# Low parts of every second weight unit by an accumulating DMA, and the C heads' softmax weights turned by VectorE and DRAM

## The chip, the cores and the metric

The kernel runs on one core of a Trainium2 chip. The metric is the device time of one execution in microseconds (us); the time before is 1841.37 us, the median of three runs (1841.23 to 1842.32). The engines are named as in the profile: PE is TensorE (PEld its weight loads), DVE is VectorE, ACT is ScalarE, POOL is GpSimd, SP is SyncE, which issues most DMAs. Each engine works through its own instructions strictly in order.

## The reference

One layer of a hybrid decoder trunk on 512 tokens of 2048 channels, all in float32, cut to what matters:

```python
h = rms_norm(x, norm1_g)
proj = h @ w_in                        # 30 tiles of 128 columns
# A: 8 heads of dilated attention; B: conv module, 512 channels (GLU, causal
#    depthwise conv of 31 taps, LayerNorm, swish); C: 16 query heads over 2 kv heads
out_b = conformer_conv(bu, bg, ...)
cq, ck = rms_norm per head
out_c = band_attention(cq, ck, cv, window 128, sinks)   # p = exp(s - max); o = p @ v / (sum p + sink)
x = x + concat(out_a, out_b, out_c) @ w_out
x = x + (silu(h2 @ w_gate) * (h2 @ w_up)) @ w_down      # h2 = rms_norm(x, norm2_g)
```

## The kernel before, in words

Activations lie transposed: channels on the 128 partitions, the 512 tokens along the free axis. Every large product is made of three products of TensorE in a rounded float32 format (`mm3`): high part of the weights by high part of the activations, high by low, and low by high. So each weight is cut into a high part `wh` and a low part `wl`, and so are the activations (`hh`, `hl` for the normed input, `mh`, `ml` for the mixed rows).

Weights come in *units* of 128 x 1024 (512 KB). Units 0 to 62 are the input projection (0 to 10 the first four column tiles, then two units for each of 26 tiles in the order of `PROJ`), the next 32 the output projection; the gate, up and down products follow. A unit goes through four steps. SyncE loads it into one of seven raw buffers (`pump`, tile `w`). ScalarE casts it to `wh`, and VectorE subtracts, `wl = w - wh` (`split_up_to`, `lows_now`); `wh` and `wl` have three buffers each. TensorE uses it: 8 slices of three matmuls, 24 in all. `next_unit()`, which the use of unit u begins with, asks for the cut of unit u+2 (`SPLIT_AHEAD`). The subtraction is deferred to a place inside the unit (`lows_now` after the fourth slice), and there, too, raw buffers are given back (`release`), one step late, and loads for them issued.

The projections set the clock of everything else: `project(name)` makes one column tile from two units and calls `ticks.tick()` after every second slice, eight ticks in a projection. `Ticks.after(n, fn)` puts a step n ticks ahead, so the order of all engines' instructions is written out by hand in ticks: the attention heads' steps, the convolution's taps on VectorE (`tap`, one multiply-add each, spaced by `TAP_TICKS` ticks for the four channel blocks), the norms. The output projection goes on ticking, and the LayerNorm of the convolution stands at tick `T_LN` = 244. The 26 projections make 208 ticks.

A C head (there are 16, in eight pairs `c0` to `c7`, started six ticks apart) goes through these steps, by the entries of `C_TICKS`: scores on TensorE into two banks of PSUM (`c0s`), masking and row maximum on VectorE (`pack`), exponentials on ScalarE into an SBUF tile `c0e` of 128 queries by 4 blocks of 128 keys (`packed_exps`), the sums (`packed_norm`), four transposes on TensorE into a bank `c0t` (`packed_flip`), the cut into a high part `c0hp` on ScalarE and a low part `c0lp` on VectorE, eight selects on GpSimd that spread both over masked tiles `c0ph`, `c0pl` (`spread_out`), and the weighing with the values on TensorE into `c0o` (`weigh`), then the copies out (`mix_c`).

Attention's V tiles are laid out without TensorE already (`do_v`): VectorE turns 32 x 32 blocks, four DMAs write them to DRAM, one reads them back.

Of the kernel before, what the change touches and what calls it, by code (L numbers as in the profile page):

```python
# [9 lines left out]
F32 = mybir.dt.float32  # L10
# [3 lines left out]
AF = mybir.ActivationFunctionType  # L14
ALU = mybir.AluOpType

P = 128
T = 512
NT = T // P
# [12 lines left out]

OUT_ORDER = (list(range(16)), [n + o for n in range(6) for o in (0, 8)] + [6, 7, 14, 15])

TAP_TICKS = (1.2, 1.3, 1.6, 1.6)
T_LN = 244
T_GLU = 14


SD, KD, VD, EV = 9, 6, 12, 1  # L40


C_TICKS = (1, 6, 2, 2, 2, 3, 5, 1, 4)
A_TICKS = (0, 8, 2, 1, 3, 1, 3, 1, 5)


# [2 lines left out]
ROWS = "c0 c1 c2 c4 c5 c3 c7 c6 a0 a1 b2 b1 b0 b3 a2 a3".split()  # L49

N_SLOTS = 73

RAW_PLAIN = "22b sb 21a 22a 11 sa 12".split()
RAW_BUFS = 8
# [62 lines left out]
def kernel(ctx: ExitStack, tc: tile.TileContext, xT, wi, wo, wgu, wd, cst_in, outT):  # L117
    nc = tc.nc
    cp = ctx.enter_context(tc.tile_pool(name="consts", bufs=1))
    wp = ctx.enter_context(tc.tile_pool(name="weights", bufs=1))  # L120
    sp = ctx.enter_context(tc.tile_pool(name="slots", bufs=N_SLOTS))
    ctx.enter_context(tc.manual_schedule())
# [13 lines left out]
    ticks = Ticks()  # L136

    def slot(name, dt=F32, cols=T):
        return sp.tile([P, cols], dt, name=name, tag="s")

    def bank(name, cols=T, pool="banks"):
        return psum[pool].tile([P, cols], F32, name=name, tag="b")


    units = [wi[0][:, :TH], wi[0][:, TH:T], wi[0][:, T:], wi[1][:, :T], wi[1][:, T:]] + [wi[u] for u in range(2, 2 * N_IN)]
# [14 lines left out]
    def drop(key):  # L160
        for buf in [b for b, k in held.items() if k == key]:
            held.pop(buf)
        return raws.pop(key)
# [42 lines left out]
    for t, (g, r) in enumerate(DOWN):  # L206
# [7 lines left out]
        for k in ("21A", "11A", "21B", "11B", "22A", "22B", "12A", "12B"):  # L214
            c = k[2]
# [17 lines left out]
    at = {"entry": 0, "split": 0, "use": 0}  # L233

    def pump(limit, most=99, eng=nc.sync):
        while at["entry"] < len(entries) and len(raws) < limit and entries[at["entry"]][0] not in held and most:
            most -= 1
            buf, key, parts = entries[at["entry"]]
            size = [part.shape[-1] * (part.shape[1] if len(part.shape) == 3 else 1) for part in parts]
            t, o = take(buf, key, sum(size)), 0  # L240
            for part, n in zip(parts, size):
                to = t[:, o:o + n]
                eng.dma_start(to.rearrange("p (n f) -> p n f", n=part.shape[1]) if len(part.shape) == 3 else to, part)
                o += n
            at["entry"] += 1


    lows, late_lows = [], []
# [8 lines left out]
    def lows_now():  # L257
        if lows and cooling:
            release()
            pump(RAW_EARLY if at["use"] <= 20 else RAW_BUFS)  # L260
        while lows:
            fn, *args = lows.pop(0)
            fn(*args)  # L263
        if late_lows and not cooling:
            pump(RAW_EARLY if at["use"] <= 20 else RAW_BUFS)

    def split_up_to(i):
        while at["split"] <= min(i, len(works) - 1):
            key, last, eng = works[at["split"]]
            of = [b for b, k in held.items() if k == key]  # L270
            t, n = drop(key) if last else raws[key]
            if cooling:
                held.update((b, None) for b in of)
                cool.extend(of)
            u = at["split"]
            hi = wp.tile([P, 1024], F32R, name=f"wh{u}", tag="hi", bufs=SPLIT_BUFS)
            lo = wp.tile([P, 1024], F32R, name=f"wl{u}", tag="lo", bufs=SPLIT_BUFS)
            if eng == "moves":

                near = psum["high"].tile([P, 1024], F32R, name=f"wn{u}", tag="h")  # L280
                src = t[:, :n].rearrange("p (n f c) -> p f n c", n=4, c=P)
                by = lambda x: x[:, :n].rearrange("p (f n c) -> p f n c", n=4, c=P)
                nc.scalar.copy(by(near), src)
                nc.scalar.copy(by(hi), src)
                nc.vector.tensor_sub(by(lo), src, by(near).bitcast(F32))
            elif eng or "high" not in psum:
                eng = eng or nc.vector

                (nc.vector.tensor_copy if u == 0 else nc.scalar.copy)(hi[:, :n], t[:, :n])  # L289
                lows.append((eng.tensor_sub, lo[:, :n], t[:, :n], hi[:, :n].bitcast(F32)))  # L290
                if not late_lows:
                    lows_now()
            else:
                near = psum["high"].tile([P, 1024], F32R, name=f"wn{u}", tag="h")
                nc.scalar.copy(near[:, :n], t[:, :n])
                nc.scalar.copy(hi[:, :n], t[:, :n])
                lows.append((nc.vector.tensor_sub, lo[:, :n], t[:, :n], near[:, :n].bitcast(F32)))
                if not late_lows:
                    lows_now()
            splits[u] = (hi, lo)  # L300
            at["split"] += 1
# [44 lines left out]
    b = bank("idle")  # L346
# [4 lines left out]
    b = idle = None  # L351
# [5 lines left out]
    ident = cp.tile([P, P], F32, name="ident")  # L357
# [137 lines left out]
    for k in range(KT):  # L495
# [21 lines left out]
        hi, lo = h_hl.pop(k)  # L517
# [287 lines left out]
    def attention(kind, box, mix, mi, heads):  # L805
        ready, every, step, s1, sx, s2, fl, ev, we = C_TICKS if kind == "c" else A_TICKS

        if mi in ROWS[-2:]:
            fl, we = fl + 2, we + 3
        name = mi  # L810
# [29 lines left out]
        def head(h):  # L840
            es = {}
            d = cp.tile([P, 3, NT], F32, name=f"{name}d{h}", tag="soft", bufs=6)
# [36 lines left out]
                nc.vector.tensor_add(den, den, mx)  # L879
                invert(h, den)  # L880

            def packed_flip():
                b = bank(f"{name}t{h}")
                for i in range(NT):
                    s = slice(i * P, (i + 1) * P)
                    nc.tensor.transpose(b[:, s], es["e"][:, s], ident)
                es.clear()
                ticks.after(ev, packed_high, b)

            def packed_high(b):  # L890
                hi = slot(f"{name}hp{h}", F32R)
# [104 lines left out]
            for u in range(len(us)):  # L996
                tu = t0 + u * step
# [7 lines left out]
            tu = t0 + (len(us) - 1) * step + s1 + sx  # L1005
            if kind == "c":
                ticks.after(tu, packed_exps)
                ticks.after(tu + s2, packed_norm)
                ticks.after(tu + s2 + fl, packed_flip)
            else:  # L1010
                for t in range(len(TBANKS[kind])):
                    ticks.after(tu + s2 + fl + t, flip, t)
# [3 lines left out]

        head(0)
        head(1)


# [12 lines left out]
    for j in range(2):  # L1033
        ticks.after(T_GLU, glu_u, j, g4[2 * j])
        ticks.after(T_GLU, glu, j, g4[2 * j + 1])
    g4 = None
    t_tap = T_GLU + 2
    for j in range(NB):
        for i in range(TAPS):
            ticks.after(int(t_tap), tap, j, i)  # L1040
            t_tap += TAP_TICKS[j]
    t_ln = T_LN
    t_ln += 2
# [12 lines left out]
    for name in PROJ[HEAD4:]:  # L1056
# [4 lines left out]
        b = project(name)  # L1061
# [17 lines left out]
    b = box = boxes = shared = None  # L1079
# [84 lines left out]
    for half in range(2):  # L1164
        for i, n in enumerate(OUT_ORDER[half]):
            if half == 1 and i == 2:
                open_banks(banks=2, high=2)
            b = bank(f"o{half}_{n}", pool="tiles")
            wh, wl = next_unit()
            for kk in range(8):  # L1170
# [4 lines left out]
                s = slice(kk * P, (kk + 1) * P)  # L1175
# [14 lines left out]
    b = m_hi = m_lo = r1b = mult_a = bias_a = bias_c = over = upper = None  # L1190
# [543 lines left out]
```

## Time and profile before

| what | us |
|---|---|
| median of three runs | 1841.37 |
| the profiled execution's own time | 1840.9 |
| its span, first to last instruction | 1839.1 |
| PE busy | 1832.4 (100%) |
| PEld busy | 1522.4 (83%) |
| DVE busy | 1428.2 (78%) |
| ACT busy | 1312.8 (71%) |
| POOL busy | 1018.3 (55%) |

In time, the first four column tiles take until 49 us, the other 26 projections with all of attention's C part and most of A's until 385 us, the output projection until 576 us; gate, up and down fill the rest. Busy time is the union of an engine's instructions; for pipelined matmuls the durations overlap (a matmul of 512 columns is listed with 0.39 us, while the next starts 0.23 us after it), so lengths on TensorE are read from start to start. In rows of the timeline the first column is the start, the second the duration, both in us; in brackets stands the idle time of the engine just ahead and what ended it. In rows by stretch, each engine's busy time is followed by its count of instructions, then the clock granted to TensorE (1.00 is full), the busy share of the 16 DMA engines, and GB/s.

### The profile page before, as it was taken

To read this page: it belongs to the slowest core of one execution; us is meant where nothing else is said; L and a number is where in the kernel's file an instruction comes from. 1 tells how busy PE (TensorE), PEld (TensorE's weight loads), DVE (VectorE), ACT (ScalarE), POOL (GpSimd) and SP (SyncE) were. 2 spreads that over 40 slices of the span, in tenths; PEclk is the share of its full clock that TensorE was granted. 3 is DMA by queue.
4 is the path that set the end of the run, shared out by engine and by line. 5 is a ranking of instruction groups with operands and counts; after the bars stand their busy time and mean duration, and the time that the engine had idled before them with its cause. 6 is when DMAs were issued, how large, how long until landed. Compare 5 with 4: busy or idle time off the path is not lost.

```text
span 1839.1 us, 26573 instructions
## 1 busy us (share of the span) xinstructions
PE 1832.4 (100%) x8319; PEld 1522.4 (83%) x8319; DVE 1428.2 (78%) x2024; ACT 1312.8 (71%) x1784; POOL 1018.3 (55%) x793
## 2 busy tenths in 40 slices
PE   9999999999999999999999999999999999999998
PEld 7888888888888888888888888888888888888887
DVE  7689888986689877777777777777777777777777
ACT  6355644553468788888888888888887778877775
POOL 0126544110003557886888767887776558776552
PEclk9999999999999999999999999999999999999999
DMA  7353255453343466777867777677687579877635
GB/s 277 89 149 122 88 144 156 111 174 120 132 138 106 113 162 182 206 206 185 223 177 211 207 185 224 175 205 208 182 271 258 199 233 283 266 255 258 237 120 109
DMA packets 401612, 337.81 MB, mean 184 GB/s; under 512 B 185408, under 2 KB 327872, under 8 KB 401472
## 3 DMA queue, kind: packets, MB, share of 16 engines
q1 hardware_dynamic: 400896, 335.33, 62.3%
q8 instruction: 66, 1.08, 0.3%
q10 hardware_dynamic: 576, 0.79, 0.1%
q14 instruction: 74, 0.61, 0.1%
HBM read 261.61 MB, written 66.03 MB: 178 GB/s over the span
## 4 chain that ended last, share of the span: by engine, by line
PE 99%; DVE 1%; DMA 0%; issue 0%; SPq 0%; ACT 0%; DVEq 0%
PE out L1315 15%; PE out L1313 15%; PE out L1316 15%; PE out L1578 7%; PE out L1579 7%; PE out L1580 7%; PE o L324 3%; PE o L323 3%; PE o L322 3%; PE cq L322 2%; PE cq L324 2%; PE cq L323 2%; PE aq L322 1%; PE ak L322 1%; PE av L322 1%; PE aq L324 1%
## 5 line engine op out<-in xcount | busy, mean ns | idle before, releaser
L1313 PE MATMUL out<-wh,h 128*128 128x512 f32 x1232 | 479.2, 389 | 0.0
L1315 PE MATMUL out<-wl,h 128*128 128x512 f32 x1232 | 479.2, 389 | 0.0
L1316 PE MATMUL out<-wh,h 128*128 128x512 f32 x1232 | 479.2, 389 | 0.0
L1313 PEld LDWEIGHTS out<-wh,h 128*128 128x128 f32 x1232 | 231.3, 188 | 48.0
L1316 PEld LDWEIGHTS out<-wh,h 128*128 128x128 f32 x1232 | 231.3, 188 | 48.0
L1315 PEld LDWEIGHTS out<-wl,h 128*128 128x128 f32 x1232 | 231.3, 188 | 47.8
L1578 PE MATMUL out<-wh,a 128*128 128x512 f32 x620 | 240.4, 388 | 0.0
L1579 PE MATMUL out<-wl,a 128*128 128x512 f32 x620 | 240.3, 388 | 0.0
L1580 PE MATMUL out<-wh,a 128*128 128x512 f32 x620 | 240.3, 388 | 0.0
L289 ACT CAST wh<-w 128x1024 fp32r<-128x1024 f32 (+2 forms) x94 | 96.9, 1031 | 138.6 <-PE o L323 49.3
L1588 DVE TENSOR_TENSOR y<-y,out 128x512 f32<-128x512 f32 x192 | 128.3, 684 | 45.4 <-PE out L1580 43.8
L263 DVE TENSOR_TENSOR wl<-w,wh 128x1024 fp32r<-128x1024 f32 (+2 forms) x95 | 114.3, 1204 | 33.5 <-ACT wh L289 33.2
L1578 PEld LDWEIGHTS out<-wh,a 128*128 128x128 f32 x620 | 116.4, 188 | 24.0
L1579 PEld LDWEIGHTS out<-wl,a 128*128 128x128 f32 x620 | 116.4, 188 | 23.8
L1580 PEld LDWEIGHTS out<-wh,a 128*128 128x128 f32 x620 | 116.4, 188 | 23.8
L582 DVE SCALAR_TENSOR_TENSOR y<-bu,cst,y 128x511 f32<-128x511 f32 (+14 forms) x120 | 89.7, 747 | 1.1
L322 PE MATMUL o<-mh_c,wh 128*128 128x512 f32 x128 | 51.0, 399 | 0.0
L322 PE MATMUL cq<-hh,wh 128*128 128x512 f32 x128 | 50.3, 393 | 0.0
L324 PE MATMUL o<-mh_c,wl 128*128 128x512 f32 x128 | 50.0, 391 | 0.0
L323 PE MATMUL o<-ml_c,wh 128*128 128x512 f32 x128 | 50.0, 390 | 0.0
L323 PE MATMUL cq<-hl,wh 128*128 128x512 f32 x128 | 49.9, 390 | 0.0
L324 PE MATMUL cq<-hh,wl 128*128 128x512 f32 x128 | 49.9, 390 | 0.0
(2357 smaller groups left out, 4741.5 us busy)
## 6 DMA issues: line engine op xcount, KB each, us to landing
od<-a SPq DMA_DIRECT2D x154, 256.0 KB
a<-od SPq DMA_DIRECT2D x154, 256.0 KB
w<-in_wi SPq DMA_DIRECT2D x58, 512.0 KB
w<-in_wo SPq DMA_DIRECT2D x32, 512.0 KB
x<-in_xT SPq DMA_DIRECT2D x16, 256.0 KB
xr<-in_xT SPq DMA_DIRECT2D x16, 256.0 KB
x2d<-xr SPq DMA_DIRECT2D x16, 256.0 KB
z<-x2d SPq DMA_DIRECT2D x64, 64.0 KB
```

Source lines behind the costliest of these rows:

```text
L263: fn(*args)
L289: (nc.vector.tensor_copy if u == 0 else nc.scalar.copy)(hi[:, :n], t[:, :n])
L322: nc.tensor.matmul(out, wh, xh, start=start, stop=False)
L323: nc.tensor.matmul(out, wh, xl, start=False, stop=False)
L324: nc.tensor.matmul(out, wl, xh, start=False, stop=stop)
L1313: nc.tensor.matmul(b, x[:, high], wh[:, s], start=c == f == 0 and q in (7, 1, 5, 2), stop=False, skip_group_check=True)
L1315: nc.tensor.matmul(b, x[:, high], wl[:, s], start=False, stop=False, skip_group_check=True)
L1316: nc.tensor.matmul(b, x[:, low], wh[:, s], start=False, stop=c == f == 1, skip_group_check=True)
L1578: nc.tensor.matmul(b[:, lo:hi], x[:, high], wh[:, s], start=start, stop=False, skip_group_check=True)
L1579: nc.tensor.matmul(b[:, lo:hi], x[:, high], wl[:, s], start=False, stop=False, skip_group_check=True)
L1580: nc.tensor.matmul(b[:, lo:hi], x[:, low], wh[:, s], start=False, stop=last, skip_group_check=True)
L1588: getattr(eng, op)(t, t, src)
```

## The change

Three things change, all in the projections and the start of the output projection.

First, for every second unit from 21 to 57 (19 units, each the first of a projection's two) VectorE's subtraction goes. ScalarE, after its cast, writes the negative rounded copy into `wl`, and GpSimd issues a DMA that reads the unit once more from DRAM and adds it to `wl`. The raw buffers are given back where a subtraction of VectorE's stands, so now once in two units.

Second, the four transposes of each C head go, and with them a bank of PSUM. VectorE turns 32 x 32 blocks of the exponentials (`packed_turn`, one tick after them), two ticks later four DMAs write them to DRAM (`packed_leave`), three ticks later one DMA reads them back into SBUF (`packed_back`), and the high cast stands five ticks after that. With `C_TICKS`' seventh entry at 7, high cast, low part, selects and weighing all stand two ticks later than before.

Third, taps lie 1.4, 1.5, 1.9 and 1.9 ticks apart and none stands from tick 205 to 214 (`T_MEET`), where the output projection begins.

```diff
-TAP_TICKS = (1.2, 1.3, 1.6, 1.6)
+TAP_TICKS = (1.4, 1.5, 1.9, 1.9)
 T_LN = 244
+T_MEET = 208
-C_TICKS = (1, 6, 2, 2, 2, 3, 5, 1, 4)
+C_TICKS = (1, 6, 2, 2, 2, 3, 7, 1, 4)
+LOWS_BY_DMA = set(range(21, 58, 2))
...
+    def complete(lo, u, n):
+        nc.gpsimd.dma_start(lo[:, :n], units[u], accum_op=ALU.add)
...
                 (nc.vector.tensor_copy if u == 0 else nc.scalar.copy)(hi[:, :n], t[:, :n])
-                lows.append((eng.tensor_sub, lo[:, :n], t[:, :n], hi[:, :n].bitcast(F32)))
+                if u in LOWS_BY_DMA:
+                    nc.scalar.activation(lo[:, :n], t[:, :n], AF.Copy, scale=-1.0)
+                    complete(lo, u, n)
+                else:
+                    lows.append((eng.tensor_sub, lo[:, :n], t[:, :n], hi[:, :n].bitcast(F32)))
...
-            def packed_flip():
-                b = bank(f"{name}t{h}")
-                for i in range(NT):
-                    s = slice(i * P, (i + 1) * P)
-                    nc.tensor.transpose(b[:, s], es["e"][:, s], ident)
-                es.clear()
-                ticks.after(ev, packed_high, b)
+            def packed_turn():
+                z = slot(f"{name}z{h}")
+                nc.vector.transpose(z, es.pop("e"))
+                ticks.after(2, packed_leave, z)
+
+            def packed_leave(z):
+                d = tc.dram_tile([T, P], F32, name=f"{name}ed{h}")
+                for a in range(4):
+                    at = slice(32 * a, 32 * a + 32)
+                    nc.sync.dma_start(d.rearrange("(n i) c -> i n c", i=32)[:, :, at],
+                                      z[at].rearrange("p (n c) -> p n c", c=32))
+                ticks.after(3, packed_back, d)
+
+            def packed_back(d):
+                t = slot(f"{name}et{h}")
+                nc.sync.dma_start(t.rearrange("p (b c) -> p b c", b=NT), d.rearrange("(b p) c -> p b c", p=P))
+                ticks.after(s2 + fl + ev - 6, packed_high, t)
...
-                ticks.after(tu + s2 + fl, packed_flip)
+                ticks.after(tu + 1, packed_turn)
...
         for i in range(TAPS):
+            if T_MEET - 3 <= t_tap < T_MEET + 7:
+                t_tap = T_MEET + 7
             ticks.after(int(t_tap), tap, j, i)
```

On TensorE, in the projection `bg2`, where before the second head of pair c3 is turned (`c3t`) and the scores of c1 (`c1s`) follow:

```order
L324 MATMUL bg_1609<-hh_192,wl_1446 128x512
L886 MATMUL c3t_1629<-ident,c3e_1473 128x128 x4
L852 MATMUL c1s_1637<-ckh_1008,cq_1140 128x256
L853 MATMUL c1s_1637<-ckl_1009,cq_1140 128x256
L852 MATMUL c1s_1637<-ckh_1008,cq_1140 128x256
L853 MATMUL c1s_1637<-ckl_1009,cq_1140 128x256
```

```order
L334 MATMUL bg_1619<-hh_192,wl_1437 128x512
L862 MATMUL c1s_1650<-ckh_1005,cq_1136 128x256
L863 MATMUL c1s_1650<-ckl_1006,cq_1136 128x256
L862 MATMUL c1s_1650<-ckh_1005,cq_1136 128x256
L863 MATMUL c1s_1650<-ckl_1006,cq_1136 128x256
```

The four transposes are gone, and the scores follow the projection's matmul directly.

On GpSimd, at the selects of the pair c0 (low parts of the first head, then high parts of the second; `cq5r` are query scales), before and after:

```order
L906 AFFINE_SELECT c0pl_1341<-c0lp_1320 128x2x128
L909 AFFINE_SELECT c0pl_1341<-c0lp_1320 128x128
L906 AFFINE_SELECT c0ph_1438<-c0hp_1421 128x2x128
L909 AFFINE_SELECT c0ph_1438<-c0hp_1421 128x2x128
L906 AFFINE_SELECT c0ph_1441<-c0hp_1421 128x2x128
```

```order
L927 AFFINE_SELECT c0pl_1386<-c0lp_1356 128x2x128
L930 AFFINE_SELECT c0pl_1386<-c0lp_1356 128x128
L271 DMA wl_1437<-in_wi 128x1024
L674 TENSOR_TENSOR cq5r<-cq5t 128x8
L675 TENSOR_TENSOR cq5r<-cq5r,c_537 128x8
L676 TENSOR_TENSOR cq5r<-cq5r,nhalf 128x8
L927 AFFINE_SELECT c0ph_1488<-c0hp_1456 128x2x128
```

The accumulating DMA of unit 29 now stands between the two heads' selects, and so do the query scales of cq5, since the selects moved two ticks.

On SyncE's queue, around the load of two weight units and the ways through DRAM of c5 and c2 (`ed` is the DRAM tile, `et` what is read back; `sums`, `by` are the heads' denominators), before and after:

```order
L243 DMA w_2051<-in_wi 128x1024
L656 DMA cq7t<-cq7d 128x16
L825 DMA c5sums<-weights_sums_559 8x32 x4
L243 DMA w_2129<-in_wi 128x1024
L243 DMA w_2212<-in_wi 128x1024
L831 DMA c5by<-c5sums 64x512 x2
```

```order
L902 DMA c5ed_2060<-c5z_2011 32x16x32 x4
L246 DMA w_2071<-in_wi 128x1024
L246 DMA w_2073<-in_wi 128x1024
L666 DMA cq7t<-cq7d 128x16
L835 DMA c5sums<-weights_sums_559 8x32 x4
L908 DMA c5et_2123<-c5ed_2060 128x4x128
L902 DMA c2ed_2188<-c2z_2147 32x16x32 x4
L246 DMA w_2230<-in_wi 128x1024
L246 DMA w_2232<-in_wi 128x1024
```

Weight loads, which stood one by one between other DMAs, stand in pairs now, behind the transfers of the turned heads.

## The prediction

> **What bounds the kernel now.** I read the page first (span, the slices, the chain that ended last), then busy time by stage, then TensorE's rows in order of time around the operations that go.
>
> ```profile
> span 1839.1 us, 26573 instructions
> PE   9999999999999999999999999999999999999998
> PE 99%; DVE 1%; DMA 0%; issue 0%; SPq 0%; ACT 0%; DVEq 0%
> ```
>
> TensorE is busy in every slice, and the chain of work is TensorE from end to end: nothing makes it wait. A time saved elsewhere is worth nothing here, and a TensorE instruction that goes is worth its full length, as long as nothing new makes TensorE wait. The change lies in the projections (49 to 385 us) and the first output units behind them. Two stretches of it, from the view of busy time by stretch:
>
> ```profile
> core 0: us, PE busy (x) PEld busy (x) DVE busy (x) ACT busy (x) POOL busy (x), PEclk, DMA share, GB/s
> 160.00:210.00 50.00, 50.00 (x266) 42.79 (x265) 47.11 (x98) 31.05 (x71) 30.64 (x47) 1.00 0.36 112
> 260.00:310.00 50.00, 50.00 (x243) 41.84 (x242) 39.52 (x74) 23.68 (x53) 21.77 (x34) 1.00 0.53 144
> ```
>
> VectorE comes next, 94% busy from 160 to 210 us; ScalarE and GpSimd are at about 60%, the DMA engines at a third to a half.
>
> **TensorE's saving.** The 16 C heads lose four transposes each: 64 instructions, in the groups by line eight rows of eight (first and last):
>
> ```profile
> L886 PE MATMUL c0t<-ident,c0e 128*128 128x128 f32 x8 | 1.2, 272 | 0.0
> ...
> L886 PE MATMUL c6t<-ident,c6e 128*128 128x128 f32 x8 | 1.2, 271 | 0.0
> ```
>
> Durations overlap in the pipeline, so I price by starts, in TensorE's timeline, once where a projection goes on behind the transposes and once where scores follow:
>
> ```profile
> 265.45 0.39 PE L324 MATMUL ak<-hh,wl 128*128 128x512 f32 x1
> 265.68 0.60 PE L886 MATMUL c4t<-ident,c4e 128*128 128x128 f32 x4
> 266.04 0.48 PE L322 MATMUL ak<-hh,wh 128*128 128x512 f32 x1
> 266.36 0.39 PE L323 MATMUL ak<-hl,wh 128*128 128x512 f32 x1
> ...
> 158.19 0.60 PE L886 MATMUL c3t<-ident,c3e 128*128 128x128 f32 x4
> 158.54 0.36 PE L852 MATMUL c1s<-ckh,cq 128*128 128x256 f32 x1
> 158.74 0.28 PE L853 MATMUL c1s<-ckl,cq 128*128 128x256 f32 x1
> 158.86 0.28 PE L852 MATMUL c1s<-ckh,cq 128*128 128x256 f32 x1
> ```
>
> Four transposes hold the array 0.35 us (265.68 to 266.04, 158.19 to 158.54). The matmul behind them holds it 0.32 us where a 512-column one takes 0.23 (265.45 to 265.68): another 0.09. Before scores the first takes 0.20 instead of 0.12: 0.08. In six groups (c7, c4, c6) a projection follows, so both parts go: 6 x 0.44 = 2.7 us. In ten, scores follow; the switch to scores stays, and how much of its 0.08 goes with the transposes no row shows: 10 x 0.35 to 0.43 = 3.5 to 4.3. Sum 6.2 to 7.0 us; I take 6.7, nearer to the upper end, since a switch without transposes ahead should cost less.
>
> **VectorE and ScalarE.** Prices from the groups and from a V tile's turn, the same operation in the same shape as the new one:
>
> ```profile
> L263 DVE TENSOR_TENSOR wl<-w,wh 128x1024 fp32r<-128x1024 f32 (+2 forms) x95 | 114.3, 1204 | 33.5 <-ACT wh L289 33.2
> L289 ACT CAST wh<-w 128x1024 fp32r<-128x1024 f32 (+2 forms) x94 | 96.9, 1031 | 138.6 <-PE o L323 49.3
> ...
> L756 DVE STREAM_TRANSPOSE av0t<-av x1: 716/716/716, 251.7 to 251.7; 128x512 f32<-128x512 f32 x1
> ```
>
> VectorE loses 19 subtractions (units 21, 23 ... 57): 19 x 1.204 = 22.9 us; it gains 16 x 0.716 = 11.5. Net 11.4 us less, and taps thin out (one per 1.4 to 1.9 ticks for 1.2 to 1.6), so some ten go to the output stage. All of that lies beside TensorE and is worth nothing in itself; it only makes VectorE's waits shorter. ScalarE gains 19 x 1.03 = 19.6 us of copies with scale -1: four in the 50 us from 160 us, 35 of 50 instead of 31, hidden by TensorE.
>
> **The low parts' deadline.** Unit u's copy is asked for when unit u-2 starts, and ScalarE gets to it when the buffer of u-3 is free; its low part is read by the third matmul of u. ScalarE's cast and TensorE's third matmul, for the shortest of the 19 (unit 21) and for unit 41 (there also the third matmul of unit 39, one projection earlier):
>
> ```profile
> 92.51 1.06 ACT L289 CAST wh<-w 128x1024 fp32r<-128x1024 f32 x1 [4.38 <-PE bu L323]
> 103.87 0.39 PE L324 MATMUL cq<-hh,wl 128*128 128x512 f32 x1
> ...
> 226.39 0.39 PE L324 MATMUL ak<-hh,wl 128*128 128x512 f32 x1
> 226.62 1.05 ACT L289 CAST wh<-w 128x1024 fp32r<-128x1024 f32 x1
> 238.72 0.39 PE L324 MATMUL av<-hh,wl 128*128 128x512 f32 x1
> ```
>
> With one more ScalarE copy (1.03) the DMA may go at 94.6 and 228.7, and is wanted at 103.9 and 238.7: 9.3 and 10.0 us. The same reading for all 19 gives 9.3 to 13.5, mean 11.3. No DMA of GpSimd's and no accumulating one stands in this trace. Nearest is a V tile's way through DRAM, 256 KB out in four and back in one, the kind of transfers the C heads gain too (SyncE's issues, GpSimd's first use, and the DMA share while they move):
>
> ```profile
> 255.81 2.27 SPq L762 DMA_DIRECT2D av0d<-av0t  x4
> 260.46 0.38 SPq L768 DMA_DIRECT2D av0s<-av0d  x1
> 263.61 1.04 POOL L773 TENSOR_TENSOR av0s<-av0s,n1w 128x512 f32<-128x512 f32 x1 [13.05 <-DMA ak0e<-ak0wide]
> ...
> 258.00:259.60 1.60, 1.60 (x9) 1.31 (x8) 1.40 (x5) 0.70 (x1) 0.00 (x0) 1.00 1.20 218
> 261.40:263.00 1.60, 1.60 (x9) 1.33 (x8) 1.53 (x3) 0.50 (x3) 0.00 (x0) 1.00 0.58 166
> ```
>
> From the end of its issue (260.84) 256 KB is usable within 2.8 us. That is the low end for 512 KB. At 166 GB/s another 256 KB adds 1.6: 4.4; if an accumulation moves its bytes twice, 512 KB more at 166 GB/s adds 3.1: 7.5; at the stage's whole 112 GB/s, 1 MB takes 9.4, with the 2.8 some 12.2, the high end. I take 4.4 to 7.5, since the share shows the engines half idle: all under 9.3, no wait, cost 0. The cover is the two units between request and use; gone, each late microsecond is TensorE's.
>
> The Trainium skill (DMA: Bandwidth & Descriptors, Anatomy of one DMA, the SWDGE path) gives 2.0 us plus bytes over 436 GB/s for a DMA from GpSimd: for 512 KB an estimate of 3.2 us, for doubled traffic 4.4. By that the deadline is kept with 5 us in hand and the sum is the same as mine; no page prices an accumulation.
>
> **Turned through DRAM.** Per head one turn on VectorE, four DMAs out two ticks later, one back after three more, the high cast five after that. A tick here is (238.72 - 226.39)/8, some 1.5 us. The V tile took 4.65 us from first issue out to issue back (three ticks: 4.6) and 3.15 to use (five ticks: 7.7). So SyncE may wait some tenths for the data out, and weight loads stand behind it; the cast on ScalarE finds its data with 4.5 us to spare. SyncE issues 16 x (2.27 + 0.38) = 42 us more over some 200: it has room. The DMA engines gain 16 x (1.2 x 1.6 + 0.58 x 1.6) = 46 us of share-time, about 0.2 on 0.36 to 0.53, and 19 accumulations on top: fuller, not full. Weight loads now go in pairs, since a buffer is only given back at a subtraction of VectorE's; they still go some 2.5 units ahead (about 16 us) against 4.4 to land. Cost 0.
>
> **GpSimd.** It issues the 19 DMAs in its order, waiting there for ScalarE's copy, and the selects that spread a head's weights stand behind; TensorE's weighing waits for those. Last select and first weighing matmul for the tightest head (c1, first) and the loosest (c7, second), then selects alone and beside VectorE, and GpSimd's small power:
>
> ```profile
> 180.63 0.28 POOL L909 TENSOR_SCALAR_AFFINE_SELECT c1pl<-c1lp 128x128 fp32r<-128x128 f32 x1
> 181.54 0.28 PE L974 MATMUL c1o<-c1ph,cv 128*128 128x256 f32 x1
> ...
> 245.12 0.28 POOL L909 TENSOR_SCALAR_AFFINE_SELECT c7pl<-c7lp 128x128 fp32r<-128x128 f32 x1
> 252.89 0.28 PE L974 MATMUL c7o<-c7ph,cv 128*128 128x256 f32 x1
> ...
> 181.66 0.40 POOL L909 TENSOR_SCALAR_AFFINE_SELECT c1ph<-c1hp 128x256 fp32r<-128x256 f32 x1
> 164.85 2.41 POOL L909 TENSOR_SCALAR_AFFINE_SELECT c3pl<-c3lp 128x256 fp32r<-128x256 f32 x1
> 227.34 1.64 POOL L666 TENSOR_TENSOR ak2wide<-ak2wide,nhalf 128x8 f32<-128x8 f32 x1
> ```
>
> Spare time is 0.6 us (180.91 to 181.54) to 7.5; five of the 16 heads have under 1.5. High cast and weighing move two ticks together, so it stays. An issue costs GpSimd between nothing (it overlaps a wait) and 2.41 us (a select stretched beside VectorE); I take 1, nearer to the plain 0.40 and the power's 1.64. Against that VectorE, whose subtractions feed the selects, is 11 us lighter. I allow 0.3 us of TensorE waits.
>
> **Sum.** 1840.9 (the profiled execution's time, 1.8 above its span) - 6.7 + 0.3 = 1834.5; the median of the runs shown, 1841.37, lies 0.5 above that execution, so 1835.0.
>
> **Rivals.** (1) GpSimd comes late. A DMA ahead of every select group at 1.64 us takes what is over the spare time of five heads (0.6, 1.1, 1.2, 1.5 and one with none): 1.0 + 0.5 + 0.4 + 0.1 + 1.6 = 3.7 us; at 2.41, some 7.5. Time 1838.4 to 1842.2. For it: the stretched selects. Against: VectorE is lighter. The Trainium skill (SBUF — State Buffer, two separate sides, the "DVE blocks DMA" box) says that GpSimd cannot write descriptors while VectorE runs certain copies in a fast mode; the rows show GpSimd held beside VectorE, though by two-input operations, and by that rule the time is this rival's. (2) The slower side: low parts land late, each of 19 units by landing time less its 9.3 to 13.5. At 10.9 us the 19 excesses sum to 6.7 and the gain is gone; at 12.2, the high end, to 20: 1835 + 20 = 1855. For it: accumulation's price is unknown and traffic grows. Against: twice the bytes still land in 7.5. (3) SyncE's waits for turned data hold the paired weight loads, casts and first matmuls come late: 16 us of lead must be lost first, then perhaps 3 to 15 us, 1838 to 1850.
>
> **Numbers.** Forecast 0.66, (1) 0.15, (2) 0.10, (3) 0.06, the rest 0.03. A measurement tells 0.2%, 3.7 us, from no change: faster is under 1837.7, slower over 1845.1. Forecast, the mild half of (1)'s doubt and a little of (3) lie under: 0.71; same 0.16; slower 0.13. The range runs from 1833.5 (7.0 saved, some run-to-run spread, no waits) to 1842.5, the far end of (1); (2) and most of (3) stay out.
>
> **What would show it.** Right: no transposes of C heads, TensorE without idle time in the projections, their end 6 to 7 us earlier (385 to about 379), later stages unchanged, VectorE under 45 of 50 us from 160 us. Wrong: TensorE waiting for a low part whose last writer is a DMA of GpSimd's (2), for GpSimd's selects (1), or for a cast behind a weight load (3).

## The result, and the profile after

The changed kernel is slower: 1861.37 us (median of 4 runs, 1859.66 to 1861.83) against 1841.3 us before (1841.04 to 1842.32), a ratio of 1.0107 with a 95% interval of 1.0095 to 1.012. That is 20 us more, where 6 us less were forecast. The profiled execution took 1861.83 us.

From the page of the kernel after: the span, TensorE's busy time, its slices, its granted clock, and the first line of the chain that ended last.

```profile
span 1859.6 us, 26638 instructions
PE 1835.3 (99%) x8255; PEld 1521.0 (82%) x8255; DVE 1422.9 (77%) x2021; ACT 1330.3 (72%) x1803; POOL 1031.6 (55%) x812
PE   9999988899999999999999999999999999999998
PEclk9999998999999999999999999999999999999999
PE 92%; DMA 2%; DVE 2%; SPq 1%; POOL 1%; issue 1%; ACT 0%; POOLq 0%; DVEq 0%; ACTq 0%
```

The 64 transposes are gone (8319 TensorE instructions before, 8255 here). But the chain is no longer TensorE from end to end: 8% of it is other engines and transfers, and slices 6 to 8 (230 to 372 us) have holes. Busy time by stretch, after:

```profile
core 0: us, PE busy (x) PEld busy (x) DVE busy (x) ACT busy (x) POOL busy (x), PEclk, DMA share, GB/s
160.00:210.00 50.00, 50.00 (x259) 42.70 (x258) 46.36 (x92) 35.10 (x77) 33.16 (x52) 1.00 0.83 200
260.00:310.00 50.00, 40.25 (x169) 32.56 (x168) 29.40 (x59) 21.12 (x44) 17.54 (x27) 0.86 0.78 188
310.00:360.00 50.00, 45.16 (x208) 37.52 (x207) 35.48 (x85) 24.88 (x45) 15.48 (x26) 0.93 0.71 179
```

From 160 to 210 us TensorE is full at clock 1.00, as forecast, though the DMA share is 0.83 where 0.36 was. From 260 to 360 us TensorE lacks 15 us, and its granted clock falls to 0.86 and 0.93. What it waited for (total, times, longest, in us):

```profile
PE aq L334 <- DMA wl<-in_wi: 5.6, 1, 5.6
PE c6o L996 <- POOL c6pl L930: 3.1, 2, 2.7
PE c4o L995 <- POOL c4ph L930: 2.2, 1, 2.2
PE c4o L996 <- POOL c4pl L930: 1.9, 1, 1.9
PE c6o L995 <- POOL c6ph L930: 1.7, 1, 1.7
```

One low part of an accumulating DMA came late (unit 47's), and the spread weights of the four heads of c4 and c6. With some smaller ones the waits come to about 16 us. The last matmul of the projections starts at 404.2 us instead of 384.5, and from there to the end the two kernels take the same time within 1 us (1455.4 and 1454.6). So 6.7 us were saved and some 26 lost: 16 of waits, and some 10 at the lowered clock behind them.

How the 5.6 us came about, on GpSimd (the scale of av0, the accumulating DMA of unit 47, the first select of c4) and on ScalarE (unit 47's negative copy), in order of time on each:

```profile
256.73 2.36 POOL L676 TENSOR_TENSOR ak0wide<-ak0wide,nhalf 128x8 f32<-128x8 f32 x1
270.65 1.04 POOL L783 TENSOR_TENSOR av0s<-av0s,n1w 128x512 f32<-128x512 f32 x1 [11.56 <-DMA av0s<-av0d]
271.63 0.91 POOL L271 DMA_DIRECT2D wl<-in_wi  x1
277.99 0.40 POOL L927 TENSOR_SCALAR_AFFINE_SELECT c4ph<-c4hp 128x256 fp32r<-128x256 f32 x1 [5.45 <-ACT c4hp L913]
...
264.69 1.07 ACT L297 ACTIVATE wl<-w 128x1024 fp32r<-128x1024 f32 x1
...
277.29 0.62 ACT L913 CAST c4hp<-c4et 128x512 fp32r<-128x512 f32 x1 [3.16 <-DMA c4et<-c4ed]
```

The copy was done at 265.76, but the DMA stands behind av0's scale in GpSimd's order, and that waited 11.56 us for av0's read-back. SyncE's queue, from which all these ways go:

```profile
260.77 2.12 SPq L841 DMA_DIRECT2D c7by<-c7sums  x2
262.99 2.21 SPq L772 DMA_DIRECT2D av0d<-av0t  x4
265.29 2.10 SPq L902 DMA_DIRECT2D c4ed<-c4z  x4
267.56 0.39 SPq L778 DMA_DIRECT2D av0s<-av0d  x1
...
272.43 3.53 SPq L902 DMA_DIRECT2D c4ed<-c4z  x4
276.07 5.35 SPq L835 DMA_DIRECT2D c4sums<-weights_sums  x4
```

Before, av0's read-back was issued at 260.46; now it goes at 267.56, right behind c4's way out. Four small issues (c4sums) took 5.35 us, where the kernel before had 1.30; one of them alone took 4.34 us, the other three 0.3 each as before. From 270 to 290 us SyncE issued 27 DMAs in 18.4 us, 0.68 each, against 25 in 12.3 before, 0.49 each; without that one long issue it is 0.54.

### The profile page after: what moved, and what is told of

Read it like the earlier page. It is cut to its first block, busy times and chain, and to the rows that moved or that the text cites. A ratio compares the mean times of both kernels' runs of the same rounds, so it can differ in the third digit from the quotient of the medians.

```text
span 1859.6 us, 26638 instructions
## 1 busy us (share of the span) xinstructions
PE 1835.3 (99%) x8255; PEld 1521.0 (82%) x8255; DVE 1422.9 (77%) x2021; ACT 1330.3 (72%) x1803; POOL 1031.6 (55%) x812
## 4 chain that ended last, share of the span: by engine, by line
PE 92%; DMA 2%; DVE 2%; SPq 1%; POOL 1%; issue 1%; ACT 0%; POOLq 0%; DVEq 0%; ACTq 0%
PE out L1339 15%; PE out L1338 15%; PE out L1336 15%; PE out L1601 7%; PE out L1602 7%; PE out L1603 7%; PE o L334 3%; PE o L332 3%; PE o L333 3%; PE cq L334 1%; PE cq L332 1%; PE cq L333 1%; PE in L334 1%; PE in L332 1%; PE in L333 1%
## 5 line engine op out<-in xcount | busy, mean ns | idle before, releaser
L266 DVE TENSOR_TENSOR wl<-w,wh 128x1024 fp32r<-128x1024 f32 (+2 forms) x76 | 91.2, 1200 | 19.6 <-ACT wh L295 19.5
L271 POOL DMA_DIRECT2D wl<-in_wi x19 | 17.2, 907 | 86.0 <-ACT wl L297 72.4
```

## The experiments

Eighteen kernels ran. Ratios are to the kernel before on the same chip, with 95% intervals. Where TensorE waits, single executions scatter by 4 to 7 us (the turn alone: 1841.6 to 1848.8), so differences of 1 or 2 us between two such kernels settle nothing.

The measure that I use throughout is TensorE's lead: the start of the same scores in each profiled execution, less that of the kernel before. Negative is ahead. The C heads' weighings stand two ticks later in TensorE's order in all of them but e2, so up to some 1 us of a lead at c4 is order and not time.

| first scores of | c4 | c6 | a0 | a1 |
|---|---|---|---|---|
| kernel before, us | 243.7 | 281.2 | 308.0 | 335.9 |
| after | -3.4 | +6.1 | +12.6 | +19.7 |
| turn alone (e1) | -5.8 | +0.1 | -0.1 | +0.6 |
| low parts alone (e2) | +0.4 | +0.4 | +0.4 | +0.4 |
| c4, c6 by TensorE (e3) | -5.2 | +2.0 | +1.7 | +2.6 |
| after without 47 (f1) | -4.5 | +3.4 | +5.0 | +17.2 |
| 12 heads, no low parts (f3) | -5.9 | +0.1 | -0.2 | +0.6 |
| no ways (h1) | -4.8 | -1.6 | -1.6 | +1.7 |
| no ways, low parts (h4) | -5.3 | -5.3 | -6.0 | +2.2 |
| single loads (i1) | -3.9 | +3.7 | +4.6 | +20.4 |

### The two halves, and two ways around SyncE

**The turn alone (e1).**

```
-LOWS_BY_DMA = set(range(21, 58, 2))
+LOWS_BY_DMA = set()
```

> All 16 C heads are turned by VectorE and laid out through DRAM as in the kernel after, but no low part is made by an accumulating DMA: units 21, 23 ... 57 get VectorE's subtraction back. Queue theory (SyncE's queue, in order, is overfull from 250 to 290 us because five issues per C head fall among the A heads' ways through DRAM; everything that waits for a transfer behind it is late): the 5.6 us wait for the low part of unit 47 goes, since no DMA stands in GpSimd's order behind the scale of av0, but the read-backs of c4 and c6 stay late and TensorE keeps 5 to 10 us of waits for their selects and the lowered clock behind them: 1838 to 1847 us. Traffic theory (the accumulations fill the 16 DMA engines and all landings stretch): waits and lowered clock go with the accumulations, 1834 to 1836 us, and the DMA share from 160 to 210 us falls from 0.83 to about 0.5.

1844.9 us, ratio 1.0021 (1.0011 to 1.003): the queue theory's outcome. The lead at c4's scores is 5.8 us; at c6's it is gone. TensorE's waits:

```profile
PE c4o L996 <- POOL c4pl L930: 3.3, 2, 3.1
...
PE c6o L996 <- POOL c6pl L930: 0.6, 1, 0.6
```

In this profiled execution (span 1840.1 us, 1.0 more than before, with 6.7 saved) 7.7 us were lost, and 3.9 us of waits do not make that up. TensorE's rows around the longest show the rest:

```profile
273.13 0.28 PE L995 MATMUL c4o<-c4ph,cv 128*128 128x256 f32 x1
276.46 0.58 PE L996 MATMUL c4o<-c4pl,cv 128*128 128x256 f32 x1 [3.06 <-POOL c4pl L930]
...
279.60 0.63 PE L334 MATMUL aq<-hh,wl 128*128 128x512 f32 x1
280.03 0.63 PE L332 MATMUL aq<-hh,wh 128*128 128x512 f32 x1
...
283.11 0.39 PE L333 MATMUL aq<-hl,wh 128*128 128x512 f32 x1
283.33 0.39 PE L334 MATMUL aq<-hh,wl 128*128 128x512 f32 x1
```

Behind the wait a 512-column matmul starts every 0.43 us instead of every 0.23, until some 282 us. A wait of 3 us costs about as much again afterwards. The Trainium skill (TensorE: Matmul & The Clock Gate, The HAM clock gate) says that the array falls to half clock after an idle window of about 3.4 us and needs as long under load to come back. The spacing here agrees (the granted clock is 0.50 from 276 to 282 us); the wait of 3.06 us is somewhat shorter than that window, and the slow stretch of nearly 6 us longer. The kernel with no ways (below) shows the same fall after idle times of 1.61 and 0.30 us with only short matmuls between and behind them, shorter still; there the measurement decides.

**The low parts alone (e2).** TensorE's transposes come back, with the old number of ticks:

```
-C_TICKS = (1, 6, 2, 2, 2, 3, 7, 1, 4)
+C_TICKS = (1, 6, 2, 2, 2, 3, 5, 1, 4)
...
-                ticks.after(tu + 1, packed_turn)
+                ticks.after(tu + s2 + fl, packed_flip)
```

> Only the other half of the change: the 19 low parts by ScalarE's negative copy and GpSimd's accumulating DMA. The C heads are turned by TensorE's transposes as before; the taps stay spread. Queue theory: SyncE has its old load, av0 is read back in time, so no low part is late; no gain from transposes either: 1840 to 1843 us, TensorE without waits of over 1 us. Traffic theory: the accumulations alone bring the waits, 1848 to 1860 us.

1842.1 us, ratio 1.0005 (0.9996 to 1.0015), and no wait over 1.1 us, none in the projections. The accumulations by themselves cost nothing that can be told from no change, though the DMA engines are as full as in the kernel after:

```profile
260.00:310.00 50.00, 50.00 (x244) 41.83 (x243) 32.65 (x68) 27.88 (x58) 19.87 (x32) 1.00 0.79 190
```

A share of 0.79 with TensorE full at clock 1.00: a full DMA side alone does not explain the loss, and the traffic theory in its plain form falls. The transfers are late here too, by less: av0's read-back is issued at 263.07 us, 2.6 later than before, and TensorE at its old pace does not feel it.

**c4 and c6 turned by TensorE (e3).**

```
+                if mi in ('c4', 'c6'):
+                    ticks.after(tu + s2 + fl, packed_flip)
+                else:
                     ticks.after(tu + 1, packed_turn)
```

> The kernel after, but the four heads of c4 and c6, which are turned between 250 and 300 us where the A heads' k and v go through DRAM too, are turned by TensorE's transposes as before. The other 12 heads go through DRAM and all 19 accumulations stay. Queue theory: SyncE's queue is short again from 250 to 290 us, the 5.6 us wait for unit 47's low part and the waits for c4's and c6's selects go, the lowered clock with them: 1841.4 - 12 x 0.42 = 1836 to 1838 us. Traffic theory: the 19 accumulations and 12 of 16 ways are still there, so most of the loss stays: 1850 to 1859 us.

1844.66 us, ratio 1.0022 (1.0012 to 1.0031). Four ways fewer take away 16.7 of the 20 us, so most of the loss needs the ways of c4 and c6; but it is no gain either. Unit 47's low part was still waited for (3.0 us), so both theories missed the size.

**Ways out from ScalarE's queue (e4).**

```
-                    nc.sync.dma_start(d.rearrange("(n i) c -> i n c", i=32)[:, :, at],
+                    nc.scalar.dma_start(d.rearrange("(n i) c -> i n c", i=32)[:, :, at],
```

> The kernel after, but the four DMAs that write a C head's turned weights to DRAM are issued from ScalarE's queue instead of SyncE's; the bytes moved are the same. Queue theory: SyncE is left with one issue per head, av0 is read back in time, the waits go: 1834 to 1838 us, unless ScalarE's 64 issues make its casts late (then a wait for a cast takes their place, 1838 to 1845). Traffic theory: same bytes, same landings, 1855 to 1863 us.

1870.6 us, ratio 1.0162 (1.0145 to 1.0179): worse than either theory said. SyncE had 21 us of issues from 250 to 290 us instead of 33.7, and yet the 5.6 us wait for unit 47 stayed and waits for c0's and c1's selects came in, ahead of 200 us. ScalarE in its turn waits for what VectorE turned, with casts and copies behind. SyncE's issue time alone is not the cause.

### One step out of the way at a time

**After without unit 47's DMA (f1); the same with c4 and c6 by TensorE (f2).**

```
-LOWS_BY_DMA = set(range(21, 58, 2))
+LOWS_BY_DMA = set(range(21, 58, 2)) - {47}
```

> The kernel after with one accumulating DMA less: unit 47, whose DMA stands in GpSimd's order behind the scale of av0, gets VectorE's subtraction back; the other 18 stay. GpSimd-order theory (that one DMA is late only because GpSimd waits 11.6 us for av0's read-back): the 5.6 us wait and some 4.5 us of lowered clock behind it go, TensorE comes to c4's selects earlier and waits there as long as in the kernel with the turn alone, or longer: 1844 to 1852 us. Traffic theory (18 of 19 accumulations fill the DMA engines as before): another unit's low part or the selects wait the more, 1855 to 1861 us.

1857.78 us, ratio 1.0089 (1.0072 to 1.0106). The wait for unit 47 went, 3.6 us came back, and waits for c6's selects grew to 9.0 us in sum. That is the traffic theory's range, not the 1844 to 1852 us of the GpSimd-order theory: GpSimd's order explains that wait and no more.

> c4 and c6 turned by TensorE, the other 12 heads through DRAM, 18 accumulations (not unit 47's). GpSimd-order theory: the 3.0 us wait for unit 47's low part and its lowered clock go, no wait over 1 us is left: 1835.5 to 1839 us, the first kernel here that beats the kernel before by 12 x 0.41 us less some tenths. Traffic theory: the wait moves to another low part or select, 1842 to 1846 us.

1843.82 us, ratio 1.0017 (1.0008 to 1.0027): a miss for the GpSimd-order theory. No wait exceeds 0.7 us, and still 4 us of small ones (c4, c7, c2, c6) are left.

**Twelve heads through DRAM, no low parts (f3).** The edits of e1 and e3 together.

> c4 and c6 turned by TensorE, the other 12 heads through DRAM, no accumulating DMA. Queue theory (the ways through DRAM hurt only where the A heads' k and v go through DRAM too, 250 to 290 us): no wait over 1 us, 1841.1 - 12 x 0.41 = 1836 to 1838 us. If the ways through DRAM hurt by themselves, wherever they are: 1839 to 1843 us.

1842.84 us, ratio 1.0009 (0.9999 to 1.0018). The queue theory said 1836 to 1838. c4's selects were waited for 3.0 us although c4 was turned by TensorE and no accumulation ran. The lateness reaches c4 without any way of its own.

**Two ticks more (f5)**, with the turn alone.

```
-C_TICKS = (1, 6, 2, 2, 2, 3, 7, 1, 4)
+C_TICKS = (1, 6, 2, 2, 2, 3, 9, 1, 4)
```

> All 16 heads through DRAM, no accumulating DMA, and two ticks (some 3 us) more between a head's read-back and its high cast, so that casts, selects and weighing of all C heads stand 2 ticks later. If the read-backs of c4 and c6 are late by a few us and no more (a fixed delay in SyncE's queue): the 3.3 us wait for c4's selects goes, 1834.5 to 1837 us. If SyncE's queue falls ever further behind, or the lateness comes from what stands ahead on GpSimd: waits of 2 us or more stay, 1839 to 1846 us.

1845.91 us, ratio 1.0026 (1.0016 to 1.0037). c4's wait went, and 6.5 us of waits for c1's and c5's selects came in its place, at 196 to 213 us: c1's cast now stands on ScalarE behind the exponentials of c5. A later tick is a later place in every queue.

**V's scale out of the way (g2 with twelve heads, g5 with all), no low parts.**

```
-            ticks.after(4, scale, vs)
+            ticks.after(11, scale, vs)
```

> Twelve heads through DRAM, c4 and c6 turned by TensorE, no accumulating DMA, and a V tile's scale stands seven ticks later, so that c4's high cast on ScalarE and its selects on GpSimd stand ahead of av0's cast and scale, which wait for av0's read-back. In-order theory (c4's selects are late only because av0's scale and casts, late from SyncE's queue, stand ahead of them on GpSimd and ScalarE): the 3.0 us wait and the lowered clock behind it go, 1836 to 1838 us. If c4's selects are late for a reason of their own: 1841 to 1844 us.

> The same later scale of V, with all 16 heads through DRAM and no accumulating DMA. In-order theory: c4's selects then wait for c4's own read-back alone; with SyncE's queue as late as it was (read-back issued at 267.0 us) they come some 2 us sooner than before: 1835 to 1839 us. If c4's own way through DRAM is what comes late: waits of 3 us or more at c4's or c6's selects stay, 1840 to 1846 us.

1841.86 us (1.0002, 0.9993 to 1.0012) and 1842.52 us (1.001, 1.0 to 1.0019). The scale moved behind c4's selects and the wait for them stayed, 3.6 and 4.0 us. In g2 the first selects did come early, at 266.0 us, but c4's low subtraction stands on VectorE behind a step of ak0 that waits 4.35 us for its read-back. Each queue has something of the A heads ahead of c4's step.

### What each part adds

**Issues alone, bytes alone, on the kernel before (g3, g4).** Both add DMAs that nobody reads, at the ways' ticks.

```
+                for a in range(4):
+                    nc.sync.dma_start(d[a:a + 1], bias_a[32 * a:32 * a + 1, :P])
...
+                nc.sync.dma_start(d.rearrange("n p c -> p n c"), bias_a.rearrange("p (n c) -> p n c", c=32))
```

> The kernel before, unchanged in its work, with five further DMAs on SyncE per C head (80 in all) at the ticks of the ways through DRAM, each of 512 B in one row, which nobody reads: the issues without the bytes. If SyncE's issue time makes the A heads' ways late: TensorE waits for c4's or c6's selects, 1843 to 1850 us. If the bytes do it (landings behind 256 KB transfers and weight loads in the same 16 rings): no wait, 1840.5 to 1842 us.

> The kernel before with two further DMAs on SyncE per C head at the same ticks, 256 KB out in packets of 128 B and 256 KB back in packets of 512 B, which nobody reads: the bytes of the ways through DRAM with two issues for five. If the bytes make the A heads' ways late: waits of 2 us or more at selects, 1843 to 1850 us. If SyncE's issue time does: under 1 us of waits, 1841 to 1842.5 us.

1841.74 us (1.0002, 0.9993 to 1.0011) and 1841.05 us (0.9998, 0.9988 to 1.0007): nothing, either way. In the kernel before, the other engines have room for either. That pointed at TensorE's pace; but these two kernels lack the later ticks of the C heads, too.

**No ways at all (h1); with issues (h2), bytes (h3), low parts (h4).** VectorE's turn stays; the five DMAs per head are left out, so the C heads' weights are not fully turned in these four kernels.

```
                 nc.vector.transpose(z, es.pop("e"))
-                ticks.after(2, packed_leave, z)
+                ticks.after(s2 + fl + ev - 1, packed_high, z)
```

> No transposes on TensorE, no accumulating DMA, and of the C heads' turn VectorE's part alone: the ten thousand small pieces are not laid out through DRAM, and the high cast reads what VectorE's turn wrote (so the weights are not fully turned: this kernel leaves out the five DMAs per head). If the DMAs of the ways make c4's selects late: no wait over 1 us, 1834 to 1836 us. If the faster TensorE by itself uses up the slack of the A heads' ways: 2 to 4 us of waits for c4's selects stay, 1838 to 1843 us.

> The kernel with no ways, with five DMAs of 512 B on SyncE per C head at the ways' ticks, which nobody reads (the C weights are not fully turned here either). If SyncE's issue time is the cause: 3 us or more above the kernel with no ways, with TensorE waiting for c4's selects. If the bytes are: within 1 us of it.

> The kernel with no ways, with two DMAs on SyncE per C head, 256 KB out in packets of 128 B and 256 KB back in packets of 512 B, which nobody reads (the C weights are not fully turned here either). If the bytes are the cause: 3 us or more above the kernel with no ways. If SyncE's issues are: within 2 us of it.

> The kernel with no ways, with the 19 low parts by accumulating DMAs as in the kernel after (the C weights are not fully turned here either). If the accumulations hurt only beside late ways, because GpSimd waits for av0's read-back ahead of unit 47's DMA: within 1.5 us of the kernel with no ways. If they hurt whenever TensorE runs at its full pace: 3 to 10 us above it.

h1: 1842.38 us, ratio 1.0005 (0.9995 to 1.0015). This is where the forecast gain goes: **with no transfer added, and the transposes gone, the kernel is no faster than before.** h2 is 1844.36 (1.0017, 1.0008 to 1.0027), h3 1844.92 (1.0021, 1.0011 to 1.003), h4 1844.09 (1.0016, 1.0006 to 1.0025): each adds about 2 us to h1, near the scatter and between what the two sides of its expectation said; h2 and h3 do not tell issues from bytes.

What holds h1 and what h4 does about it, in the last matmul of av's projection, VectorE's turn of it, and the stretch; first the kernel before (its turn stands at 251.7), then h1:

```profile
251.30 0.39 PE L324 MATMUL av<-hh,wl 128*128 128x512 f32 x1
210.00:260.00 50.00, 50.00 (x262) 42.65 (x261) 41.42 (x85) 24.25 (x54) 21.26 (x43) 1.00 0.42 112
```

```profile
247.41 0.39 PE L334 MATMUL av<-hh,wl 128*128 128x512 f32 x1
251.69 0.70 DVE L766 STREAM_TRANSPOSE av0t<-av 128x512 f32<-128x512 f32 x1
210.00:260.00 50.00, 49.27 (x247) 41.49 (x246) 47.37 (x94) 27.96 (x69) 33.04 (x50) 1.00 0.43 110
PE c4o L983 <- POOL c4pl L917: 1.9, 2, 1.6
PE c6o L983 <- POOL c6pl L917: 1.9, 1, 1.9
```

The projection ends 3.9 us earlier than before, and VectorE turns it at the same time as before (251.7): it is busy 47.4 of 50 us, where the kernel before had 41.4. The lead stops at VectorE, and on SyncE the step falls behind the kernel before. The rows that lead from there to c4's selects, before (c7by alone) and in h1:

```profile
245.88 1.09 SPq L831 DMA_DIRECT2D c7by<-c7sums  x2
```

```profile
256.47 1.18 SPq L841 DMA_DIRECT2D c7by<-c7sums  x2
...
258.37 2.27 SPq L772 DMA_DIRECT2D av0d<-av0t  x4
263.81 0.38 SPq L778 DMA_DIRECT2D av0s<-av0d  x1
...
267.87 0.71 ACT L789 CAST av<-av0s 128x256 fp32r<-128x256 f32 x2 [5.66 <-POOL av0s L783]
...
270.29 0.62 ACT L900 CAST c4hp<-c4z 128x512 fp32r<-128x512 f32 x1
```

av0's way out is issued 2.6 us later than before (258.37 for 255.81) and its read-back 3.4 (263.81 for 260.46), and c4's high cast stands on ScalarE behind av's, which waits for it. About half of the 2.6 is VectorE's (ak2's low parts, which SyncE sends first, went at 251.79 for 250.47); the other half is c7by, which stood ahead of ak2's parts before and now, with the C heads two ticks later, stands between them and av0. So h1's loss is not TensorE's pace alone. The same read-back is late by 4.2 us in e1, 4.5 in f3 and 7.1 in the kernel after.

Now h4, where VectorE is rid of the subtractions:

```profile
246.92 0.39 PE L334 MATMUL av<-hh,wl 128*128 128x512 f32 x1
247.63 0.70 DVE L766 STREAM_TRANSPOSE av0t<-av 128x512 f32<-128x512 f32 x1
259.73 0.38 SPq L778 DMA_DIRECT2D av0s<-av0d  x1
210.00:260.00 50.00, 49.47 (x249) 41.94 (x248) 41.85 (x84) 27.91 (x64) 26.84 (x47) 1.00 0.70 154
PE c6o L983 <- POOL c6pl L917: 3.1, 2, 2.7
PE c6o L982 <- POOL c6ph L917: 2.8, 1, 2.8
321.92 0.58 ACT L991 COPY mix_c<-c6o 64x512 f32<-64x512 f32 x1 [6.24 <-DMA ak1h<-ak1hi]
```

The turn follows its projection at once, av0's read-back is issued 0.7 us earlier than before (of 4.1 gained at the turn, the rest is lost in SyncE's queue), c4's wait is gone, and TensorE keeps its lead of 5 to 6 us as far as a0's scores. Then c6's selects are late: ScalarE waited 6.24 us for ak1's transfer, which took 7.8 us in the chain of work. So the accumulations relieve VectorE in this kernel, and what is late then comes late by the transfers; that the accumulations' own traffic does it was not separated.

**Weight loads one by one (i1, i2).** Buffers go back at each unit; i2 has ten heads through DRAM (c4, c6 and c7 by TensorE) and 18 accumulations besides.

```
-    def lows_now():
-        if lows and cooling:
+    def lows_now(half=False):
+        if cooling and (lows or half):
```

> The kernel after, with raw weight buffers given back at every unit instead of at every second one, so that weight loads go one by one as in the kernel before; 16 ways and 19 accumulations stay. Pairs theory (a 1 MB burst of two loads ahead of the A heads' small transfers on the same rings and in SyncE's queue makes the ways late): the waits for unit 47's low part and for c4's and c6's selects shrink by half or more, 1844 to 1852 us. If pairs do not matter (the sum of bytes and issues does): 1857 to 1863 us.

> Ten heads (c0, c1, c2, c3, c5) through DRAM, c4, c6 and c7 turned by TensorE, 18 accumulations (not unit 47's), weight loads one by one. VectorE is relieved of 18 subtractions and no way through DRAM falls behind 225 us. If the A heads' stretch from 225 to 330 us is where all is lost: no wait over 1 us, 1841.1 - 10 x 0.41 = 1837 to 1838.5 us. If TensorE meets the other engines wherever it gets ahead: 1840 to 1843 us.

1862.52 us (1.0114, 1.0099 to 1.013) and 1842.77 us (1.0008, 0.9998 to 1.0017). The pairs theory falls. In i2 the waits in the A heads' stretch are small, and 4.1 us saved are still given back, part of it early: unit 21's low part was 1.3 us late.

No version beats the kernel before by what a measurement can tell.

## Why the prediction was wrong, by its own steps

- **TensorE's saving, 6.7 us: right.** In the turn alone the lead grew to 4.0 us over the first ten groups (up to 222 us), 0.40 each, inside the 0.35 to 0.44 priced; with the low parts by DMA and no ways TensorE was still 6.0 us ahead at a0's scores.
- **"A TensorE instruction that goes is worth its full length": this is the step that failed first, by the term "0.3 us of TensorE waits".** The kernel after has some 16 us of them, and some 10 us more at lowered clock behind. The full length held only for as long as every later hand-off had more spare time than TensorE gained. I read GpSimd's spare times (0.6 to 7.5 us; c4's second head, the "one with none", had begun its weighing at 286.24 us, ahead of its last select's end at 286.98) against a TensorE at its old pace and took them as fixed: "high cast and weighing move two ticks together, so it stays". For c4's first head the rows of the kernel before give the second and the last select of its low part, and the two matmuls that wait for them (the first and the third of `c4pl`):

```profile
271.82 0.85 POOL L909 TENSOR_SCALAR_AFFINE_SELECT c4pl<-c4lp 128x256 fp32r<-128x256 f32 x1
...
273.97 0.70 POOL L909 TENSOR_SCALAR_AFFINE_SELECT c4pl<-c4lp 128x128 fp32r<-128x128 f32 x1
...
276.26 0.28 PE L975 MATMUL c4o<-c4pl,cv 128*128 128x256 f32 x1
...
276.75 0.28 PE L975 MATMUL c4o<-c4pl,cv 128*128 128x256 f32 x1
```

  That is 3.6 us of spare at the second select (272.67 to 276.26) and 2.1 at the last (274.67 to 276.75). In the kernel with no ways TensorE came to this weighing 2.1 us earlier (274.02 for 276.15, its place being two ticks later in the order), and the second select ended 3.2 us later (275.85): 1.7 short, and TensorE waited 1.61. In the turn alone it is 3.0 earlier (273.13) and 3.7 later (276.40): 3.1 short, and the wait was 3.06. The forecast needed the selects to come earlier with TensorE; they came later, behind av0's way.
- **"All of that lies beside TensorE" (VectorE): wrong where VectorE keeps the subtractions, and no protection in the kernel after.** In h1 VectorE, at 47 busy of 50 us, turned av0 4.3 us after its projection's last matmul. In h4, lighter as forecast, it turned it at once. In the kernel after it was light as well (38.4 of 50 us from 210 us), and yet the turn came 6.2 us after that matmul (254.99 for 248.76), because VectorE itself waited for ak2's read-back:

```profile
248.72 0.75 DVE L742 SCALAR_TENSOR_TENSOR ak2k<-ak2raw,gqk,ak2wide 128x512 f32<-128x512 f32 x1 [5.35 <-DMA ak2wide<-ak2e]
```

- **"Turned through DRAM", cost 0, "it has room": wrong in the cost, not in the sum.** The 42 us of issues over 200 would add 8.5 in 40; from 250 to 290 us SyncE had 24.4 us of issues before, 33.7 after and 33.5 in the turn alone. But an in-order queue that is full for over 80% of a stretch and waits for others' data besides was late all the same: with low parts by DMA, av0's read-back went out 7.1 us later than before. The price per issue, 0.38 to 0.57 us, held on the mean but for the one of 4.34. Rival (3) named SyncE, but with the wrong victim: not weight loads and casts of units, but the A heads' ways and what stands behind them on GpSimd, ScalarE and VectorE.
- **The low parts' deadline: the landing was right in the main** (5.1 to 9.3 us from the start of the issue, median 5.4, against 4.4 to 7.5 taken; six of 19 took 8.1 or more), and in the profiled execution all but unit 47's came within 0.2 us of need. The lead of unit 47 was read with av0's scale at its old time; the DMA was issued 5.9 us after its data was ready. The price of the Trainium skill (DMA: Bandwidth & Descriptors, Anatomy of one DMA, SWDGE path), an estimate of 3.2 us for the bytes once or 4.4 twice, lies below the measured 5.4.
- **Waits priced at their length: mis-sized.** Some 10 us of the loss is TensorE at half pace behind 16 us of waits. The far ends of rivals (1) and (3), 1842 and 1850, fell short for that too.
- **Later stages unchanged: right** within 1 us.

What stays open is why the two parts together cost so much: ways and accumulations each add about 2 us to the kernel with no ways, together 19. It takes c4's and c6's ways (e3), it takes the accumulations (e1), 3.6 us of it is unit 47 (f1), and pairs of loads are not it (i1). Late read-backs from SyncE's queue fit; what makes them so late when both parts are there was not shown. h1 also has VectorE's 16 turns and the C heads' steps two ticks later in every queue, so how much of its loss is the pace alone was not separated: a kernel with TensorE's transposes kept and only the ticks moved was not run. The fall of c4's wait in h4 shows VectorE's share.

## What to carry to other kernels

When work is taken off the engine that bounds, subtract the time gained so far from the spare time of every later hand-off; the first that turns negative is where the gain ends. Ask for each whether the step that feeds it comes earlier too, or stands behind a transfer that does not. Look for the second-fullest engine in that stretch, and for in-order queues in which the late step stands behind another chain's wait: moving one such step only shows the next. A wait of some us on TensorE is to be priced at up to twice its length.

## What the runs showed of the hardware

- Behind TensorE's waits of 1.9 us (1.61 and 0.30, h1) to 5.6 us (after), 512-column matmuls started every 0.43 us instead of 0.23 for some 3 to 5 us; behind one of 1.3 us (i2) they did not.
- An accumulating DMA from GpSimd: 0.907 us of issue, 512 KB landed in 5.4 us (median of 19). From 160 to 210 us its packets of 4 KB took 328 ns (median), plain ones 159.
- Issues on SyncE from 270 to 290 us took 0.49 us each before (DMA share 0.56), 0.52 with the low parts alone (0.86) and 0.68 after (0.73), most of the last by one issue of 4.34 us: the share does not set it.
